# A fixed TensorE order for the attention of a two-block network: fillers, turns, values, next scores

## The chip, the cores and the metric

The kernel runs on one core of a Trainium2 chip. Its time is device microseconds for one execution, and the median over a few runs is what counts. Before the change the median was 1479.84 us (three runs, 1479.53 to 1481.19). The engines are named as the profile names them: PE is TensorE (matrix multiplies), DVE is VectorE, ACT is ScalarE, POOL is GpSimd, and SP is the engine that issues the loads.

## The reference

The network is two blocks of two layers each, on one sequence of 256 tokens with 1024 channels. The change touches the first block, whose two layers each compute this, cut to what matters:

```
mod = silu(c) @ ada_w + ada_b
sh_m, sc_m, gt_m, sh_f, sc_f, gt_f = split(mod, 6)
h = rms_norm(x) * (1 + sc_m) + sh_m
aq, ak, av, bq, ..., cqkv, cz, ca, cb = split(h @ w_in)
o_a = banded_attention(rope(aq), rope(ak), av, window 128, sinks)
o_b = nsa_mixer(...)        # compressed + selected + window branches, gated
o_c = gated_delta_net(conv(cqkv), ca, cb, cz)   # per chunk a solve, then a scan over chunks
x = x + gt_m * (concat(o_a, o_b, o_c) @ w_out)
h = rms_norm(x) * (1 + sc_f) + sh_f
x = x + gt_f * ((silu(h @ w_gate) * (h @ w_up)) @ w_down)
```

Every tensor is fp32. `ada_w` is 1024 x 6144 for each layer, so modulation is a product of one vector with a large matrix. Inputs pass through unchanged by the change described here; only the order of the work, its buffers and the engine of a few operations differ.

## The kernel before

**Splitting.** Every large fp32 product is computed as three multiplies of split parts (high by high, high by low, low by high). `cut` (L188) makes the two parts of a weight tile of 128x1024: `wh` by a copy on ACT (L193), and `wl` by a subtraction on DVE or POOL (L194). One projection block, `pf` (`proj_fm`, L209 to L211), is then 24 matmuls of 128x256 into PSUM.

**Loads.** `load` (L183) issues on SP. Nearly all weights go through one ring of three staging buffers named `ws`, 1 MB each. SP issues its loads in a fixed order, and a load whose staging buffer is still in use holds back all loads behind it.

**Modulation.** `mod_unit` (L342) loads 1 MB of `ada_w` into that same ring and reduces it on DVE with two operations of 128x1024 (L350). The units for layer 0 and 1 are done piece by piece by calls of `pump` among other work.

**The mixer of the first block** (`mixer1`) first makes the projections of seven heads while DVE, ACT, POOL and PE work on the triangular solve of the gated delta net. Then comes the attention. A pair of heads goes through: scores `sc` (L383, PE); maximum and exponentials `lg` (L394 on DVE, L399 on ACT) and the scaling by the reciprocal of the sum (L404 on DVE, L411 on ACT); three transposes for each head, `tp` (L419, PE), copied to SBUF as `pt` (L421, ACT); and the product with the values, `ot` (L429, L431, PE). There are six such pairs in a layer: two for banded attention (`aq0`, `aq1`), four for the window and selected branches (`bq0`, `bq1` against two key sets). Eight projection blocks (numbers 4 to 11 of `w_fm`) stand among them; each feeds a short convolution `gdn_conv` (copy `cu` L716, taps L725 to L730 on ACT and DVE, then transposes `vp` L736 or sums `ssp` L748 on PE). A projection `pz` (24 steps of 128x512, twice) ends the stage, and after it comes the scan over chunks (`gdn_scan`, first DVE instruction L879).

**What sets the order.** The framework's scheduler orders every engine's instructions by program position and readiness, so before the change the projection blocks are spread between the pieces of the attention wherever the scheduler found a place for them. Each engine executes its own list in order, and waits on semaphores of the others.

**Between the layers**, `begin1` normalizes the input of layer 1 with `norm`: for each of eight tiles `h = x * rb` (L303), scale and shift (L305 or L307), the high part `hh` (ACT, L308) and the low part `hl` (L309). POOL has seven of the multiplies and one `hl`.

Of the kernel before, what the change touches and what calls it, by code (L numbers as in the profile page):

```python
# [8 lines left out]
F32 = mybir.dt.float32  # L9
# [133 lines left out]
class Net:  # L143
# [44 lines left out]
    def cut(self, ws, pool=None, tag="w", bufs=6, eng=None):  # L188
# [34 lines left out]
    def proj_tm(self, outs, src, n, pre=None):  # L223

        mm = self.nc.tensor.matmul
        for k in range(0, KT, 2):
# [3 lines left out]
            for tb in range(2):  # L230
                t = slice(tb * P, tb * P + P)
                for i in range(2):
# [3 lines left out]
                    mm(outs[tb], lhsT=self.hh[k + i][:, t], rhs=wl[:, i, :], start=False, stop=last)  # L236

# [101 lines left out]
    def mod_load(self, l, u, sp=None):  # L339
        return self.load(self.io["ada_w"][l, u], (P, 2, 1024), sp, bufs=3 if sp is None else 4)  # L340

    def mod_unit(self, l, u, sp=None, aw=None):  # L342

        nc = self.nc
        if aw is None:
# [168 lines left out]
    def begin1(self, w_fm, pp):  # L514
# [3 lines left out]
        self.norm(range(KT), self.gmod[:, 1, 0, :], self.mod[:, 1, 0:8], range(1, 8), (5, 6, 7), (7,))  # L518
# [6 lines left out]
    def mixer1(self, l, begin, turn):  # L525
        nc, tc, io = self.nc, self.tc, self.io
        with ExitStack() as ctx:
# [11 lines left out]
            def conv(i0, blocks):  # L539
                for j, ps in enumerate(blocks):  # L540
                    if i0 > 2:
                        flush()
                    late.append(self.gdn_conv(l, sp, pp, g, i0 + j, ps))
                    if j % 2:
                        self.pump((3 if i0 == 4 and j == 1 else 1) if l == 0 and i0 > 2 else 0)
# [3 lines left out]
            conv(0, ahead)  # L549
# [62 lines left out]
            two = []  # L612

            def values():

                pts = [self.turned(sp, pp, u[1]) for u in two]
                self.pv([(out, pt, *rest) for (out, _, *rest), pt in zip(two, pts)])
                two.clear()


            bandq0, bandq1 = self.c(C_BAND, 128), self.c(C_BAND + 128, 256)
            for blk in range(2):
                ot = pp.tile([P, S], F32, tag="o", name="ot", bufs=1)
                sc = self.scores(pp, rot[f"aq{blk}"], self.kk[2])
                for half in range(2):
                    h = blk + 2 * half
# [953 lines left out]
```

## Time and profile before

| | |
|---|---|
| median of three runs | 1479.84 us |
| time of the profiled execution | 1485.39 us |
| its span | 1483.6 us |
| PE busy | 1416.1 us, 95% |
| DVE busy | 1137.7 us, 77% |
| ACT busy | 824.0 us, 56% |
| POOL busy | 122.5 us, 8% |
| mean granted TensorE clock | 0.98 |

The profiled execution has 1.8 us outside the span, and its time is 5.55 us above the median of the runs. The engines' busy time is an average over stages with different limits. The attention of layer 0 lies between about 105 and 198 us of the span, that of layer 1 between about 507 and 573 us, and the normalization at the start of layer 1 between about 424 and 446 us.

### The profile page before, as it was taken

The numbers are of one execution on the slowest core, as the hardware profiler recorded it, in microseconds if no ns is written. First come the engines' busy times: TensorE is split into PE (matmuls) and PEld (weight loads), VectorE is DVE, ScalarE is ACT, GpSimd is POOL, SyncE is SP. The second block draws the span as 40 slices with busy tenths as digits, with TensorE's granted clock in tenths as the row PEclk, the third lists the DMA queues.
The fourth block names the chain that finished last, engine by engine and source line by source line (L and its number), as shares of the span: only waits on it lengthen the run. The fifth ranks groups of instructions, "written<-read, shape, count | busy, mean of one in ns | idle before, by whom it ended". The sixth has DMA issues, their size and how long they took to land.

```text
span 1483.6 us, 29119 instructions
## 1 busy us (share of the span) xinstructions
PE 1416.1 (95%) x11742; PEld 1322.0 (89%) x11742; DVE 1137.7 (77%) x2352; ACT 824.0 (56%) x1585; POOL 122.5 (8%) x130
## 2 busy tenths in 40 slices
PE   5987999999999999999999999999999999899998
PEld 3865789999998778999999888899999888899997
DVE  7868789989868576975667886797888675887875
ACT  3634766445465586554446555665555654755554
POOL 0130101000042300100001001100000100100000
PEclk9997999999999999999999999999999999999999
DMA  9555457989732522779744443279664341655520
GB/s 374 200 199 212 168 192 296 359 312 346 287 105 93 200 86 103 271 264 160 285 163 146 142 143 142 99 277 228 249 230 139 116 144 56 252 214 201 187 86 29
DMA packets 52504, 287.77 MB, mean 194 GB/s; under 512 B 6061, under 2 KB 12081, under 8 KB 24466
## 3 DMA queue, kind: packets, MB, share of 16 engines
q1 hardware_dynamic: 50962, 279.62, 51.6%
q0 software_dynamic: 1408, 6.29, 3.5%
q8 instruction: 92, 1.51, 0.4%
q14 instruction: 42, 0.34, 0.1%
HBM read 277.97 MB, written 7.34 MB: 192 GB/s over the span
## 4 chain that ended last, share of the span: by engine, by line
PE 77%; DVE 12%; ACT 5%; issue 2%; POOL 2%; DMA 2%; POOLq 0%; SPq 0%; DVEq 0%; ACTq 0%
PE pf L209 15%; PE pf L210 14%; PE pf L211 14%; PE acc L209 5%; PE acc L211 5%; PE acc L210 5%; DVE ws L350 2%; DVE wl L194 2%; PE sc L383 2%; PE ot L429 2%; PE tp L419 1%; ACT wh L193 1%; DVE hl L205 1%; POOL sq L67 1%; PE zp L829 1%
## 5 line engine op out<-in xcount | busy, mean ns | idle before, releaser
L209 PE MATMUL pf<-hh,wh 128*128 128x256 f32 (+1 forms) x1976 | 566.8, 287 | 7.1 <-ACT wh L193 5.7
L210 PE MATMUL pf<-hl,wh 128*128 128x256 f32 (+1 forms) x1976 | 564.3, 286 | 6.3 <-DVE hl L205 6.3
L211 PE MATMUL pf<-hh,wl 128*128 128x256 f32 (+1 forms) x1976 | 562.6, 285 | 0.2 <-DVE wl L194 0.2
L194 DVE TENSOR_TENSOR wl<-ws,wh 128x1024 fp32r<-128x1024 f32 (+1 forms) x289 | 349.2, 1212 | 76.1 <-ACT wh L193 73.9
L193 ACT CAST wh<-ws 128x1024 fp32r<-128x1024 f32 (+1 forms) x299 | 306.8, 1036 | 180.6 <-PE pf L210 133.7
L209 PEld LDWEIGHTS pf<-hh,wh 128*128 128x128 f32 x1976 | 378.0, 192 | 15.2 <-ACT wh L193 6.5
L210 PEld LDWEIGHTS pf<-hl,wh 128*128 128x128 f32 x1976 | 378.6, 192 | 12.5 <-DVE hl L205 9.6
L211 PEld LDWEIGHTS pf<-hh,wl 128*128 128x128 f32 x1976 | 378.2, 192 | 2.4 <-issue 1.8
L211 PE MATMUL acc<-ah,dl 128*128 128x256 f32 x704 | 198.2, 282 | 0.0
L210 PE MATMUL acc<-al,dh 128*128 128x256 f32 x704 | 198.0, 282 | 0.0
L209 PE MATMUL acc<-ah,dh 128*128 128x256 f32 x704 | 197.7, 283 | 0.2
L194 DVE TENSOR_TENSOR dl<-wd,dh 128x1024 fp32r<-128x1024 f32 x88 | 107.6, 1223 | 50.6 <-ACT dh L193 50.3
L193 ACT CAST dh<-wd 128x1024 fp32r<-128x1024 f32 x88 | 91.9, 1049 | 94.4 <-PE acc L210 89.1
L210 PEld LDWEIGHTS acc<-al,dh 128*128 128x128 f32 x704 | 133.8, 190 | 0.2
L211 PEld LDWEIGHTS acc<-ah,dl 128*128 128x128 f32 x704 | 133.7, 190 | 0.0
L209 PEld LDWEIGHTS acc<-ah,dh 128*128 128x128 f32 x704 | 132.9, 190 | 0.7 <-ACT ah L201 0.6
L350 DVE SCALAR_TENSOR_TENSOR ws<-ws,sc 128x1024 f32<-128x1024 f32 x96 | 116.0, 1222 | 5.3 <-ACT sc L475 5.3
L67 POOL TENSOR_TENSOR sq<-sq 128x256 f32<-128x256 f32 x52 | 44.5, 855 | 774.0 <-ACT sq L65 768.3
L1119 DVE SCALAR_TENSOR_TENSOR fy<-fu,cw,fy 128x255 f32<-128x255 f32 (+1 forms) x176 | 84.1, 481 | 5.7 <-ACT fy L1117 3.0
L1100 DVE TENSOR_TENSOR a<-pf,rb 128x258 f32<-128x258 f32 x88 | 37.2, 424 | 32.2 <-PE pf L211 29.9
L399 ACT ACTIVATE lg<-lg,st 128x128 f32<-128x128 f32 x112 | 50.1, 449 | 21.2 <-DVE st L394 17.7
L1117 ACT ACTIVATE fy<-fu,cw 128x256 f32<-128x256 f32 x88 | 52.6, 599 | 12.1 <-DVE fu L1116 12.0
(370 smaller groups left out, 2143.3 us busy)
## 6 DMA issues: line engine op xcount, KB each, us to landing
ws<-in_ada_w SPq DMA_DIRECT2D x48, 1024.0 KB, 5.2
ws<-in_w_gu SPq DMA_DIRECT2D x44, 1024.0 KB, 5.2
wd<-in_w_dn SPq DMA_DIRECT2D x44, 1024.0 KB, 6.3
ws<-in_w_up SPq DMA_DIRECT2D x44, 1024.0 KB, 5.0
ws<-in_w_fm SPq DMA_DIRECT2D x16, 1024.0 KB, 5.1
ws<-in_w_even SPq DMA_DIRECT2D x12, 1024.0 KB, 4.9
w<-in_cmp_w SPq DMA_DIRECT2D x8, 1024.0 KB, 4.8
ws<-in_w_out SPq DMA_DIRECT2D x8, 1024.0 KB, 4.8
```

The source lines that it names most:

```text
L67: (nc.vector if i else nc.gpsimd).tensor_tensor(sq, sq, last, op=ALU.add)
L193: nc.scalar.copy(wh, ws)
L194: (eng or nc.vector).tensor_tensor(wl, ws, wh.bitcast(F32), op=ALU.subtract)
L209: mm(out, lhsT=lh, rhs=rh, start=start, stop=False, **kw)
L210: mm(out, lhsT=lh, rhs=rl, start=False, stop=False, **kw)
L211: mm(out, lhsT=ll, rhs=rh, start=False, stop=stop, **kw)
L350: nc.vector.scalar_tensor_tensor(a, a, 1.0, self.sc, op0=ALU.mult, op1=ALU.mult, accum_out=acc)
L383: self.nc.tensor.matmul(sc[half][:, out], lhsT=q[r, t], rhs=k[r, 0:n], start=True, stop=True)
L399: nc.scalar.activation(lg[:, rng[i]], lg[:, rng[i]], AF.Exp, bias=nm[:, i:i + 1], scale=-1.0, accum_out=den[:, i:i + 1])
L1100: nc.vector.tensor_tensor(t[j], ps[j], self.rb, op=ALU.mult)
L1117: nc.scalar.activation(y, u, AF.Identity, scale=w[:, 2:3], bias=w[:, 3:4])
L1119: nc.vector.scalar_tensor_tensor(y[:, d:S], u[:, 0:S - d], w[:, 2 - d:3 - d], y[:, d:S], op0=ALU.mult, op1=ALU.add)
```

## The change

The attention is written as six steps inside a region where the scheduler keeps PE's instructions in program order (`manual_schedule`). Each step is two fillers (a filler is a projection block of 24 matmuls, or a quarter of the two `pz` accumulations), then the turning of the pair's probabilities, the transposes of late convolutions, the values, and the next pair's scores. Modulation takes its 1 MB in two halves of 512 KB, through a ring `aw` of three buffers of its own; the ring of cut weights goes from six to five buffers, and the units are taken in another order. The compressed branch is split into its scores and its turning. In `begin1`, POOL multiplies three tiles and not seven, and no `hl`.

```
-    def cut(self, ws, pool=None, tag="w", bufs=6, eng=None):
+    def cut(self, ws, pool=None, tag="w", bufs=5, eng=None):
...
         for i in range(2):
             m = 2 * u + i
-            a, acc = aw[:, i, :], self.mod[:, l, m:m + 1]
+            a = self.load(self.io["ada_w"][l, u, :, i], (P, 1024), tag="aw") if aw is None else aw[:, i, :]
+            acc = self.mod[:, l, m:m + 1]
...
-        self.norm(range(KT), self.gmod[:, 1, 0, :], self.mod[:, 1, 0:8], range(1, 8), (5, 6, 7), (7,))
+        self.norm(range(KT), self.gmod[:, 1, 0, :], self.mod[:, 1, 0:8], (1, 3, 5), (5, 6, 7), ())
...
             self.cmp_mlp(l, sp, pp, g)
+            ws[4] = self.load_blocks(w_fm, 4)
             self.pump(2 if l == 0 else 0)
-            ws[4] = self.load_blocks(w_fm, 4)
...
+            def fills():
+                for i in range(4, 12, 2):
+                    for j, ps in enumerate(self.blocks(w_fm, i, pool=(1,), ws=ws.get(i))):
+                        late.append(self.gdn_conv(l, sp, pp, g, i + j, ps))
+                        yield
+                pz.extend(self.pj.tile([P, 512], F32, tag="pj", name="pz") for _ in range(2))
+                yield from self.proj_tm_steps(pz, io["w_z"][l], 512)
+
+            fill, pc = fills(), None
+            with tc.manual_schedule(engines={nc.tensor.engine}):
+                lgs = attend(0)
+                for i in range(6):
+                    for _ in range(2):
+                        next(fill)
+                    if i == 0:
+                        cmp = self.cmp_probs(sp, pp, g, raw)
+                    pts = [self.turned(sp, pp, lg) for lg in lgs]
+                    if i == 1:
+                        pc = cmp()
+                    for one in late[0:2 * min(i, 1)]:
+                        late.pop(0)()
+                    if i in (0, 1, 2, 4):
+                        ot = pp.tile([P, S], F32, tag="o", name="ot", bufs=1)
+                    value(i, pts, ot, pc)
+                    if i < 5:
+                        lgs = attend(i + 1)
+                        self.pump(2 if l == 0 else 0)
...
-        self.pump_list = [lambda l=l, u=u: self.mod_unit(l, u) for l in range(2) for u in range(8 * (1 - l), 24)]
+        units = [(0, u) for u in range(8, 20)] + [(1, u) for u in range(8)] + [(0, u) for u in range(20, 24)]
+        units += [(1, u) for u in range(8, 24)]
+        self.pump_list = [lambda l=l, u=u: self.mod_unit(l, u) for l, u in units]
```

Removed are the loops that computed the six pairs one after the other with their own `values()`, and `conv`, which took the projection blocks in two groups of four with one convolution behind each and pumped 2, 2, 3, 1, 1 and 1 units beside the 2 before them; `attend(i)` makes pair i's scores and probabilities, and `value(i, ...)` its products with the same calls as before.

Three places show what moved. The first is PE in layer 0, around the end of the first pair. Before, the pair's transposes (`tp`), the next scores (`sc`) and the values (`ot`) stand between single matmuls of a projection block (`pf`):

```order
L419 MATMUL tp<-ident,lg 128x128
L383 MATMUL sc<-kk_90,rotaq_802 128x128
L419 MATMUL tp<-ident,lg 128x128 x2
L383 MATMUL sc<-kk_90,rotaq_802 128x256
L211 MATMUL pf<-hh_72,wl 128x256
L209 MATMUL pf<-hh_73,wh 128x256
L429 MATMUL ot<-pt,vt_457 64x256
L431 MATMUL ot<-pt,vt_460 64x128 x2
```

On PE of the changed kernel, the same place and the end of the following step, the line numbers being those of the new source:

```order
L425 MATMUL tp<-ident,lg 128x128 x6
L435 MATMUL ot<-pt,vt_457 64x256 x2
L437 MATMUL ot<-pt,vt_460 64x128 x2
L389 MATMUL sc<-kk_90,rotaq_802 128x128 x2
L389 MATMUL sc<-kk_90,rotaq_802 128x256 x2
...
L425 MATMUL tp<-ident,lg 128x128 x6
L1055 MATMUL ctp<-ident,ce 64x128 x2
L751 MATMUL vp<-ident,cv 128x128 x4
L435 MATMUL ot<-pt,vt_457 64x256 x2
```

Between the two (at the line of dots) stand 48 `pf` matmuls without a break; all six transposes of a pair are together, and its four value products follow.

The second place is DVE in layer 0 after the first projection blocks. Before, the modulation operations (L350) of three units follow one another, with the compressed branch (`ce`) behind them:

```order
L350 SCALAR_TENSOR_TENSOR ws,mod<-ws,sc 128x1024
L730 SCALAR_TENSOR_TENSOR cv<-cu,cv 128x256
L202 TENSOR_TENSOR ol_123<-ot,oh_115 128x256
L730 SCALAR_TENSOR_TENSOR cv<-cu,cv 128x256
L350 SCALAR_TENSOR_TENSOR ws,mod<-ws,sc 128x1024 x2
L353 TENSOR_TENSOR mod<-mod,adab 128x2
L350 SCALAR_TENSOR_TENSOR ws,mod<-ws,sc 128x1024 x2
L353 TENSOR_TENSOR mod<-mod,adab 128x2
L350 SCALAR_TENSOR_TENSOR ws,mod<-ws,sc 128x1024
L1024 TENSOR_TENSOR ce<-cp,cs 128x64
```

On DVE of the changed kernel in the second step, L356 is the modulation, L409 and L410 are the sums and reciprocals of the probabilities, and L742 the taps of a convolution:

```order
L356 SCALAR_TENSOR_TENSOR aw,mod<-aw,sc 128x1024
L409 TENSOR_TENSOR st<-st 128x2
L403 TENSOR_SCALAR st<-st,nsink 128x2
L410 RECIPROCAL st<-st 128x2
L356 SCALAR_TENSOR_TENSOR aw,mod<-aw,sc 128x1024
L194 TENSOR_TENSOR wl<-ws,wh 128x1024
L359 TENSOR_TENSOR mod<-mod,adab 128x2
L356 SCALAR_TENSOR_TENSOR aw,mod<-aw,sc 128x1024
L409 TENSOR_TENSOR st<-st 128x2
L742 SCALAR_TENSOR_TENSOR cv<-cu,cw,cv 128x255
L410 RECIPROCAL st<-st 128x2
```

The modulation operations now stand singly between the pieces of the probabilities and the convolutions. From the first pair's probabilities to the scan's first instruction there are 20 of them before and 22 after; ahead of that stretch there are 20 before and 25 after.

The third place is SP's loads in the same stage. Before:

```order
L976 DMA w_1244<-in_cmp_w 128x2048
L185 DMA ws<-in_ada_w 128x2048 x2
L185 DMA ws<-in_w_fm 128x2x1024
L185 DMA ws<-in_ada_w 128x2048 x7
L185 DMA ws<-in_w_fm 128x2x1024
L185 DMA ws<-in_ada_w 128x2048
```

On SP of the changed kernel, where `aw` is the new ring and each of its loads is half as large:

```order
L185 DMA aw<-in_ada_w 128x1024 x6
L991 DMA w_1244<-in_cmp_w 128x2048
L185 DMA ws<-in_w_fm 128x2x1024
L185 DMA aw<-in_ada_w 128x1024
L185 DMA ws<-in_w_fm 128x2x1024
L185 DMA aw<-in_ada_w 128x1024 x3
L185 DMA ws<-in_w_fm 128x2x1024
```

The second load of projection weights stood behind seven loads of 1 MB in the same ring; it now stands behind one of 512 KB in another ring.

## Rows read from the trace of the kernel before

**Rows 1.** The page's first part: span, and busy time of each engine.

```profile
span 1483.6 us, 29119 instructions
PE 1416.1 (95%) x11742; PEld 1322.0 (89%) x11742; DVE 1137.7 (77%) x2352; ACT 824.0 (56%) x1585; POOL 122.5 (8%) x130
```

**Rows 2.** Busy time by stretches, layer 0's attention; columns in the first row.

```profile
core 0: us, PE busy (x) PEld busy (x) DVE busy (x) ACT busy (x) POOL busy (x), PEclk, DMA share, GB/s
120.00:130.00 10.00, 7.60 (x48) 5.42 (x47) 7.64 (x28) 6.76 (x25) 0.00 (x0) 1.00 0.60 205
130.00:140.00 10.00, 6.30 (x23) 3.64 (x22) 7.05 (x18) 4.05 (x12) 0.00 (x0) 0.52 0.36 125
140.00:150.00 10.00, 6.16 (x36) 5.87 (x37) 9.97 (x31) 3.36 (x7) 2.46 (x1) 0.62 0.88 337
150.00:160.00 10.00, 7.49 (x49) 6.51 (x49) 9.86 (x27) 6.73 (x19) 2.37 (x1) 0.89 0.75 265
160.00:170.00 10.00, 10.00 (x73) 8.52 (x71) 7.75 (x26) 7.36 (x23) 2.39 (x1) 0.94 0.69 220
```

**Rows 3.** PE's instructions in time: start, duration, engine, line; idle before, releaser.

```profile
128.43 0.84 PE L419 MATMUL tp<-ident,lg 128*128 128x128 f32 x3 [1.73 <-ACT lg L411]
143.69 0.58 PE L209 MATMUL pf<-hh,wh 128*128 128x256 f32 x1 [5.75 <-ACT wh L193]
...
145.44 0.41 PE L209 MATMUL pf<-hh,wh 128*128 128x256 f32 x1
145.66 0.41 PE L210 MATMUL pf<-hl,wh 128*128 128x256 f32 x1
...
150.78 0.28 PE L209 MATMUL pf<-hh,wh 128*128 128x256 f32 x1
150.90 0.28 PE L210 MATMUL pf<-hl,wh 128*128 128x256 f32 x1
...
156.55 0.33 PE L736 MATMUL vp<-ident,cv 128*128 128x128 f32 x1 [2.51 <-DVE cv L730]
```

**Rows 4.** ACT's instructions in time, at the weight cut that PE awaits.

```profile
142.59 1.99 ACT L193 CAST wh<-ws 128x1024 fp32r<-128x1024 f32 x2 [1.07 <-DMA ws<-in_w_fm]
```

**Rows 5.** SP's loads in time.

```profile
98.90 29.63 SPq L185 DMA_DIRECT2D ws<-in_ada_w  x7
137.65 0.38 SPq L185 DMA_DIRECT2D ws<-in_w_fm  x1
```

**Rows 6.** DVE's instructions in time: first probabilities, modulation, first of the scan.

```profile
106.80 0.27 DVE L394 CUSTOM_DVE_ANT_0 lg<-sc,cs 128x128 f32<-128x128 f32 x1
...
136.39 1.22 DVE L350 SCALAR_TENSOR_TENSOR ws<-ws,sc 128x1024 f32<-128x1024 f32 x1
...
141.12 1.22 DVE L350 SCALAR_TENSOR_TENSOR ws<-ws,sc 128x1024 f32<-128x1024 f32 x1
...
197.96 1.39 DVE L879 SCALAR_TENSOR_TENSOR dec<-qp,gcols,dec 128x128 f32<-128x128 f32 x5
```

**Rows 7.** Busy time by stretches: the whole attention of layer 0, then of layer 1.

```profile
106.80:197.96 91.16, 78.28 (x606) 61.66 (x601) 72.97 (x212) 58.39 (x164) 11.04 (x6) 0.89 0.56 194
507.15:573.00 65.85, 64.94 (x429) 50.70 (x428) 44.14 (x142) 53.24 (x149) 7.20 (x3) 1.00 0.34 121
```

**Rows 8.** DMA issues from 78 to 200 us: count, size, median us to landing.

```profile
ws<-in_ada_w SPq DMA_DIRECT2D x12, 1024.0 KB, 5.0
```

**Rows 9.** POOL's instructions in time, at the start of layer 1.

```profile
439.70 2.63 POOL L303 TENSOR_TENSOR h<-x,rb 128x256 f32<-128x256 f32 x2 [1.70 <-DVE hl L309]
```

**Rows 10.** PE's instructions in time, start of layer 1.

```profile
443.30 0.39 PE L234 MATMUL pm<-wh,hh 128*128 128x276 f32 x1 [1.82 <-ACT hh L308]
```

**Rows 11.** Busy time by stretches, elsewhere; columns as in rows 2.

```profile
440.00:450.00 10.00, 8.09 (x49) 7.44 (x48) 7.67 (x17) 8.73 (x18) 3.06 (x3) 0.83 0.18 54
470.00:480.00 10.00, 7.99 (x62) 7.38 (x61) 6.83 (x17) 2.36 (x6) 1.82 (x2) 0.83 0.03 6
```

**Rows 12.** PE's instructions in time, attention of layer 1.

```profile
516.29 0.33 PE L419 MATMUL tp<-ident,lg 128*128 128x128 f32 x1 [0.91 <-ACT lg L411]
```

More of the change, by code (lines that the diff above doesn't have):

```diff
@@ L336, in two_norms, with mod_load @@
         return gg, g1, e2
-    def mod_load(self, l, u, sp=None):
-        return self.load(self.io["ada_w"][l, u], (P, 2, 1024), sp, bufs=3 if sp is None else 4)
+    def mod_load(self, l, u, sp):
+        return self.load(self.io["ada_w"][l, u], (P, 2, 1024), sp, bufs=4)
     def mod_unit(self, l, u, sp=None, aw=None):
         nc = self.nc
-        if aw is None:
+        if aw is None and sp is not None:
             aw = self.mod_load(l, u, sp)
@@ L537, in flush @@
                     late.pop(0)()
[L539 to L545, printed above, removed]
             g = {"kT": [], "qT": []}
             g["ssq"], g["ssk"] = sp.tile([P, 8], F32, name="gssq"), sp.tile([P, 8], F32, name="gssk")
-            conv(0, ahead)
+            for j, ps in enumerate(ahead):
+                late.append(self.gdn_conv(l, sp, pp, g, j, ps))
             pre, ws = None, {}
@@ L609, in mixer1 @@
             self.cmp_mlp(l, sp, pp, g)
+            ws[4] = self.load_blocks(w_fm, 4)
             self.pump(2 if l == 0 else 0)
-            ws[4] = self.load_blocks(w_fm, 4)
[L612 to L626, printed above, removed]
-                    lg = self.probs(sp, sc[half], bandq0, bandq1,
-                                    nsink=self.nsink[:, l, h:h + 1], sink=self.sink[:, l, h:h + 1])
-                    r = slice(64 * half, 64 * half + 64)
-                    two.append((ot[r, :], lg, vt[0][:, r], vt[1][:, r], True, True))
-                values()
-                self.pump(2 if l == 0 else 0)
-                self.split(ot, oh[blk], ol[blk])
@@ L634, in mixer1 @@
-            conv(4, (ps for i in (4, 6) for ps in self.blocks(w_fm, i, pool=(1,), ws=ws.get(i))))
-            pc = self.cmp_probs(sp, pp, g, raw)
-            c0, c1 = self.c(C_CAUS, 128), self.c(C_CAUS + 128, 256)
-            for blk in range(2):
-                ot = pp.tile([P, S], F32, tag="o", name="ot", bufs=1)
-                nc.tensor.matmul(ot, lhsT=g["v2"][:, 2 * blk:2 * blk + 2, :].rearrange("p h d -> p (h d)"), rhs=pc,
-                                 start=True, stop=False, skip_group_check=True)
-                for br in range(2):
-                    sc = self.scores(pp, rot[f"bq{blk}"], self.kk[br])
-                    for half in range(2):
-                        h = 2 * blk + half
-                        r = slice(64 * half, 64 * half + 64)
-                        lg = self.probs(sp, sc[half], c0, c1, gate=g["gates"][:, :, 4 * (br + 1) + h])
-                        vs = slice(128 + 64 * br, 192 + 64 * br)
-                        two.append((ot[r, :], lg, vt[0][:, vs], vt[1][:, vs], False, br == 1))
-                    values()
-                self.split(ot, oh[2 + blk], ol[2 + blk])
@@ new lines, in value @@
+            def value(i, pts, ot, pc):
+                blk, br = divmod(i - 2, 2)
+                if i >= 2 and br == 0:
+                    nc.tensor.matmul(ot, lhsT=v2[:, 2 * blk:2 * blk + 2, :].rearrange("p h d -> p (h d)"), rhs=pc,
+                                     start=True, stop=False, skip_group_check=True)
+                two = []
+                for n, pt in enumerate(pts):
+                    r = slice(64 * n, 64 * n + 64)
+                    vs = r if i < 2 else slice(128 + 64 * br, 192 + 64 * br)
+                    two.append((ot[r, :], pt, vt[0][:, vs], vt[1][:, vs], i < 2, i < 2 or br == 1))
+                self.pv(two)
+                if i < 2 or br == 1:
+                    n = i if i < 2 else 2 + blk
+                    self.split(ot, oh[n], ol[n])
```

35 lines of the change are left out of this document (26 added, 9 removed).

## The prediction

> **What bounds the kernel now.** I read the page first: PE is busy 1416.1 of 1483.6 us [rows 1], so it idles 67 us in all, and a change in the order of its work can give back only part of that. Which part, the table of 10 us stretches tells. In layer 0's attention PE is busy 7.60, 6.30, 6.16 and 7.49 us of four stretches in a row [rows 2], 27.55 of 40, so 12.45 us of idle time lie there, the largest hole that the change touches. The reader should look at DVE in the same rows: it is at 7 to 7.6 us of ten while the hole opens and at 9.97 and 9.86 in its second half. It is late rather than free.
>
> PE's instructions in order of time say what ended the idle time [rows 3]: 1.73 us before a pair's transposes, until ACT had scaled the probabilities; 5.75 us before a projection block, until ACT had cut its weights; 2.51 us before the transposes of a convolution, until DVE had finished it. For the longest, one step back: ACT had waited for the load of those weights [rows 4]. SP's list shows why the load was late. Seven modulation loads were issued from 98.90 us on over 29.63 us, because each needs a staging buffer that DVE must first empty, and the projection weights went out only at 137.65 us [rows 5]. The operations that empty them are the five that start from 136.39 to 141.12 us, 1.22 us each [rows 6]. So PE waited for weights, and the weights for modulation.
>
> The hole has a second price. The granted clock is 0.52 and 0.62 in two of these stretches. The reader can see its price in the starts of matmuls of 128x256: 0.22 us apart after 145.44 us and 0.12 us after 150.78 us [rows 3]. Counting each stretch's busy time times what its clock lacks gives 6.30 x 0.48 + 6.16 x 0.38 + 7.49 x 0.11 + 10 x 0.06, about 6.8 us. A perfect order would thus save 12.45 + 6.8, some 19 us, if nothing else were late.
>
> **Part 1, layer 0's attention: -12 us (-15 to +3).** What is late next is DVE. From the first probabilities at 106.80 us to the scan's first DVE instruction at 197.96 us [rows 6] are 91.16 us, of which DVE is busy 72.97 and PE 78.28 [rows 7]. PE's work at full clock is 78.28 less 6.8, 71.5 us. DVE's grows: the order has 22 modulation operations where 20 stood, so 72.97 + 2 x 1.22 = 75.4 us. DVE has become the longer of the two, and how fully it can be used decides. Before, it was 72.97/91.16, 80% busy. Where it was the bound, from 140 to 160 us, it was 99% busy [rows 2]. The new order helps it: modulation has its own buffers, so an operation that finds its data ready fills DVE's gaps singly; the weights stand behind one half-load where they stood behind seven. But each pair is still a chain through PE, DVE, ACT and PE again, and DVE takes its list in order. I take 95%, nearer to the stretch where it was the bound: 75.4/0.95 = 79.4 us, so 11.8 us less. At 99% it is 76.2 (-15), at 80% 94.3 (+3). Both ends stay in the range.
>
> Three things in this part I cost at nothing beyond that. Five more modulation operations stand before the first probabilities (25 for 20), 6.1 us of DVE beside the solve; the trace has one such operation in a round of the solve without a longer round, and DVE's share above leaves room for the rest; if not, +2. The solve's last rounds lose the single projection matmuls that stood between them, which then follow in one piece. And 512 KB loads cost more issues on SP, which issues nothing else that is urgent there.
>
> **Part 2, layer 0's scan and output projection: +1 (-1 to +6).** About five modulation operations now stand among the scan's DVE instructions, which are themselves a chain with PE. At 1.22 us each [rows 6] that is 6.1 us if each delays the chain, nothing if each fits a wait. The scan has waits on PE in each round, so I take 1. Later modulation is the less by as many, for which I take -0.5 at the feed-forward part that follows, so +0.5 together.
>
> **Part 3, the start of layer 1: -2 (-3 to +1).** PE waits 1.82 us at 443.30 us for ACT's last high part [rows 10], which stands at the end of a chain through POOL: its two multiplies at 439.70 us take 2.63 us [rows 9]. The stretch is 1.91 us short of busy at a granted clock of 0.83 [rows 11], so wait and clock together are worth 1.91 + 8.09 x 0.17, 3.3 us. With three tiles on POOL the last tiles come from DVE. DVE gets four more multiplies and one more low part, at 7.67 us busy of ten [rows 11], which keeps a little of the wait. Were DVE the later of the two, it could cost 1.
>
> **Part 4, layer 1's attention: +3 (0 to +6).** There is nothing to win here: PE is busy 64.94 of 65.85 us at full clock, while DVE has 44.14 and ACT 53.24 [rows 7]. The single wait is 0.91 us at a pair's transposes [rows 12]. A fixed order can only add. In each step the six transposes wait for both heads' probabilities, and the whole queue of PE stands behind them (values, next scores, fillers); the scheduler had put a filler matmul there. The fillers of a step, 48 matmuls at 0.12 us, 5.8 us, cover a chain of DVE and ACT whose busy time is (44.14 + 53.24)/6 = 16 us a step, partly side by side; so the cover is not sure. A step that fails by the 0.91 seen costs 6 x 0.91 = 5.5 us. I take 0.5 a step, 3 us, as some steps will be covered.
>
> **Part 5, five buffers for cut weights and not six: 0 to +1**; elsewhere PE is at 95% and more, and a ring of five still holds two weight tiles beyond the one in use. I take +0.5.
>
> **Sum.** -11.8 + 0.5 - 2 + 3 + 0.5 = -9.8 us. The profiled execution took 1485.39 us, so the new one 1475.6; the median of the runs is 5.55 us under that, hence 1470.
>
> A rule of the skill speaks against part 1's small loads. The trace's 1 MB modulation loads landed after 5.0 us in the median [rows 8], and nothing here shows a load of half the size. The Trainium skill, "DMA: Bandwidth & Descriptors", section "Bandwidth", says to batch transfers to at least 1 MiB for three quarters of the peak; by its fit in the section "Anatomy of one DMA" (2.0 us and the bytes at 436 GB/s) two halves would take an estimated 6.4 us one after the other where one whole takes 4.4. By that rule the second rival below would be likelier; by the trace, in which the DMA engines are between 0.36 and 0.88 busy in these stretches, halves can overlap.
>
> **The rivals.**
>
> *DVE is not held by data but PE and ACT are held by each other (slower).* In layer 0's attention each engine waits for the next in a fixed circle, and DVE stays 80% busy: +3. Layer 1 loses its 0.91 at each step, +5.5; the other parts stay at -1. Together +7.5: 1487. For it speaks that PE's longest list now waits on one condition, and that a hole lowers the clock: a stretch with 7.99 us of PE's ten has a clock of 0.83 [rows 11]. Against it, that 120 to 130 us with 7.60 still has 1.00 [rows 2] and that fillers are now 48 in one piece. It decides, with layer 1 at +5.5, when DVE falls below 75.4/(91.16 - 4.5) = 87% of layer 0's stretch. The Trainium skill, "TensorE: Matmul & The Clock Gate", section "A second HAM failure mode: psum-queue depth-cycling", says that short idle times between groups of matmuls make the clock swing between its two levels; the two rows just named show it once and once not.
>
> *The ring of three halves paces modulation, or the weights stay late (no change).* A half is reduced in 1.22 us, but its buffer is full again only after a load, at most the 5.0 us of a whole one [rows 8]. Three in flight give one half per 1.67 us; a burst of four in a step would wait some 1.5 us, five steps 7.5 us of DVE. And the weights of blocks 4 and 5 do stand behind six half-loads. Layer 0 then gains 4.5 and the sum is -2.5: 1477.
>
> *Everything fits (larger gain).* DVE at 99%, -15; the scan 0; begin -3.3; layer 1 0: -18, 1462. For it speaks that ACT and PE have room in layer 0 (58.39 of 91.16 busy for ACT); against it, 99% over 90 us.
>
> **How the numbers follow.** The forecast has a chance of 0.50, the larger gain 0.18, the ring 0.20, the slower one 0.12. A measurement of this kernel cannot tell 0.2%, 3 us, from no change: faster is below 1476.9, slower above 1482.8. The forecast's own bounds (layer 0 -8 to -14, layer 1 0 to +5) are 1464 to 1476, faster in nearly all. The ring case is half on each side of 1476.9. So faster is 0.49 + 0.18 + 0.10 = 0.77, the same 0.01 + 0.10 + 0.01 = 0.12, slower 0.11. The range 1460 to 1480 holds the forecast, the ring and most of the larger gain, and leaves out the slower case and the gains beyond 20 us.
>
> **What would show it.** The first probabilities of layer 0 stay near 107 us and the scan's first DVE instruction comes at 186 us, with DVE 95% busy between and PE's clock near 1. No projection block waits 5 us for its cut weights, and SP issues the weights of the second pair of blocks well before they are cut. PE's waits move to `tp` and `ot`, up to 2 us each in layer 0. Layer 1's attention ends some 3 us later after its start, with short waits at `tp`. The wait of 1.82 us at `pm` is gone. The prediction is wrong if DVE shows holes of more than 1.5 us in front of modulation (then the ring paces it), if PE's clock stays below 0.9 in layer 0, or if layer 1 loses more than 6 us.

## The result: slower, and the profile after

The changed kernel takes 1490.88 us in the median (four runs, 1489.77 to 1496.11) against 1480.11 for the kernel before in the same comparison: a ratio of 1.007, 95% interval 1.0049 to 1.009. In a second comparison, beside other variants, it was 1.0062 (1.0045 to 1.0079). The forecast was 1470, faster; the time lies outside its range.

A second profile of each kernel was taken, since a single execution can mislead: the profile of before that stands ahead of the prediction is 5.5 us above the median of its runs, and a second one took 1476.23 us. The table gives both profiles of each kernel. The marks are the starts of DVE's first probabilities and of the scan's first DVE instruction, and the starts of PE's last matmuls of the output projections and feed-forward parts and of its first `pm` in layer 1.

| stretch | before, two profiles | after, two profiles | mean change | forecast |
|---|---|---|---|---|
| start to layer 0's first probabilities | 106.8, 106.5 | 113.9, 113.9 | +7.2 | 0 |
| from there to the scan | 91.2, 89.4 | 84.9, 83.5 | -6.1 | -11.8 |
| scan to the end of the output projection | 32.0, 32.0 | 36.0, 34.9 | +3.5 | +0.5, with what follows |
| layer 1: first `pm` to first probabilities | 73.1, 73.1 | 72.0, 71.7 | -1.3 | -2 |
| layer 1: probabilities to the scan | 65.3, 65.3 | 69.7, 69.7 | +4.4 | +3 |
| layer 1: end of output projection to end of feed-forward | 197.4, 193.4 | 200.6, 201.2 | +5.5 | +0.5 (five buffers) |
| second block, first probabilities to PE's end | 613.0, 609.8 | 606.4, 607.7 | -4.3 | 0 |

Two terms carry the miss: up to layer 0's scan the two first rows add to +1.1 where -11.8 was forecast, and the feed-forward row has +5.5 where +0.5 was. The -4.3 in the second block is in part that of one long execution of before (see e9).

The page's first part answers to [rows 1]; PE is still at 95%, so nothing of the loss is seen there.

```profile
span 1488.2 us, 29207 instructions
PE 1411.2 (95%) x11742; PEld 1320.1 (89%) x11742; DVE 1143.7 (77%) x2357; ACT 823.2 (55%) x1585; POOL 121.6 (8%) x125
```

The stretches show it. First layer 0's solve and attention by 10 us, then the whole attention of layer 0 and of layer 1 of the changed kernel; the columns are those of [rows 2].

```profile
100.00:110.00 10.00, 7.51 (x142) 6.19 (x138) 9.96 (x13) 5.64 (x14) 9.09 (x5) 0.91 0.95 346
110.00:120.00 10.00, 10.00 (x135) 8.24 (x133) 6.05 (x20) 2.08 (x5) 1.96 (x3) 0.50 0.49 156
140.00:150.00 10.00, 4.66 (x30) 3.66 (x29) 10.00 (x23) 7.31 (x24) 2.66 (x1) 0.79 0.60 199
150.00:160.00 10.00, 8.72 (x56) 6.42 (x55) 8.24 (x26) 6.55 (x21) 0.00 (x0) 0.70 0.45 171
160.00:170.00 10.00, 7.85 (x49) 5.39 (x48) 8.97 (x26) 7.46 (x21) 0.00 (x0) 0.83 0.90 325
113.90:198.85 84.95, 74.86 (x627) 60.84 (x628) 75.26 (x221) 56.87 (x168) 6.50 (x3) 0.87 0.66 232
512.71:582.41 69.70, 61.95 (x409) 50.59 (x409) 40.81 (x137) 51.65 (x147) 4.71 (x2) 0.90 0.27 93
```

The hole in layer 0 has moved, not closed: 4.66 us of PE from 140 to 150 us where [rows 2] had 6.16, and a new one in the solve from 100 to 110 us, with the clock at its lower level (0.50) for the 10 us behind it. Most of the new one is a single wait of PE for DVE:

```profile
106.42 0.37 PE L1012 MATMUL ckp<-hth,kw 128*128 128x16 f32 x2 [2.17 <-DVE hth L1007]
```

Layer 1, which had 0.91 us of idle PE at clock 1.00 [rows 7], now has 7.75 at 0.90. And DVE is as full as 9.96 and 10.00 where PE waits.

What DVE did in the new holes: its instructions in time, in the solve and in the attention's second step.

```profile
100.38 1.22 DVE L194 TENSOR_TENSOR wl<-ws,wh 128x1024 fp32r<-128x1024 f32 x1
101.51 3.38 DVE L356 SCALAR_TENSOR_TENSOR aw<-aw,sc 128x1024 f32<-128x1024 f32 x1
104.82 0.41 DVE L858 TENSOR_TENSOR xx<-xx,zp 128x256 f32<-128x256 f32 x1
106.55 3.38 DVE L194 TENSOR_TENSOR wl<-ws,wh 128x1024 fp32r<-128x1024 f32 x1
142.92 3.36 DVE L194 TENSOR_TENSOR wl<-ws,wh 128x1024 fp32r<-128x1024 f32 x1
146.27 1.21 DVE L356 SCALAR_TENSOR_TENSOR aw<-aw,sc 128x1024 f32<-128x1024 f32 x1
147.88 0.15 DVE L410 RECIPROCAL st<-st 128x2 f32<-128x2 f32 x1
```

Three operations took 3.36 to 3.38 us where operations of the same forms take 1.22: the cut at 100.38, and modulation in [rows 6]. POOL's instructions of the same times:

```profile
100.63 3.18 POOL L194 TENSOR_TENSOR wl<-ws,wh 128x1024 fp32r<-128x1024 f32 x1 [1.75 <-ACT wh L193]
103.76 2.40 POOL L849 TENSOR_TENSOR ms<-md,lv 128x256 f32<-128x256 f32 x2
106.45 2.40 POOL L194 TENSOR_TENSOR wl<-ws,wh 128x1024 fp32r<-128x1024 f32 x1 [0.29 <-ACT wh L193]
...
142.54 2.66 POOL L194 TENSOR_TENSOR wl<-ws,wh 128x1024 fp32r<-128x1024 f32 x1 [8.46 <-PE pf L211]
```

Each stretched operation starts while POOL cuts a weight and ends about one operation's own time (1.2 us) after POOL does: POOL ends at 103.81, 108.85 and 145.20, DVE at 104.89, 109.93 and 146.28. All three read both operands from SBUF. The operation at 104.82 reads one from PSUM (`zp`) and kept its 0.41 us beside POOL's next work. It goes the other way too: POOL's cut at 100.63 began while DVE made its own cut of 100.38, and took 3.18 us where the one at 106.45 took 2.40. The Trainium skill, "SBUF — State Buffer", section "Who interferes with whom", says that a DVE instruction with two SBUF inputs contends with a GpSimd instruction that reads SBUF, and that the second to come blocks until the first is done; these rows agree, with 2.2 us a time. It is a rule that the prediction should have weighed. The trace of before had it in small, an operation of 128x2 on DVE that took 2.33 us beside POOL's cut:

```profile
144.66 2.46 POOL L194 TENSOR_TENSOR wl<-ws,wh 128x1024 fp32r<-128x1024 f32 x1 [34.03 <-ACT wh L193]
...
144.81 2.33 DVE L113 TENSOR_TENSOR hl<-mod,hh 128x2 fp32r<-128x2 f32 x1
```

What stood behind: ACT's instruction that waits for the reciprocal, then PE's in layer 0 and layer 1.

```profile
148.13 0.80 ACT L417 ACTIVATE lg<-lg,st 128x128 f32<-128x128 f32 x2 [2.10 <-DVE st L410]
```

```profile
148.59 1.09 PE L425 MATMUL tp<-ident,lg 128*128 128x128 f32 x3 [4.93 <-ACT lg L417]
...
163.84 0.44 PE L751 MATMUL vp<-ident,cv 128*128 128x128 f32 x2 [1.12 <-ACT vs L752]
165.31 0.33 PE L751 MATMUL vp<-ident,cv 128*128 128x128 f32 x1 [1.02 <-ACT vs L752]
...
446.22 0.39 PE L238 MATMUL pm<-wh,hh 128*128 128x276 f32 x1 [0.51 <-ACT hh L313]
...
531.53 0.88 PE L425 MATMUL tp<-ident,lg 128*128 128x128 f32 x2 [2.01 <-ACT lg L417]
549.10 0.44 PE L751 MATMUL vp<-ident,cv 128*128 128x128 f32 x2 [2.00 <-ACT vs L752]
```

The chain in layer 0 reads: POOL's cut stretches DVE's cut by some 2.1 us, a modulation operation of 1.21 us and a convolution tap follow, the reciprocal of a head's sum comes at 147.88, ACT scales at 148.13, and PE, whose order has the transposes first, waited 4.93 us. Behind these transposes stood the pair's values, which need them, but also the next scores and 48 filler matmuls, which do not; the fillers' first weights were cut by 146.28, so they could have filled only the end of this wait. The wait of 5.75 us [rows 3] for cut weights is gone, as was forecast, and one of 4.93 stands in its place. In layer 1 the waits are the same without modulation, shorter and more of them. The wait at `pm` [rows 10] fell from 1.82 to 0.51.

### The profile page after: what moved, and what is told of

Same layout as the page of the kernel before. It is cut to its first block, busy times and chain, and to the rows that moved or that the text cites. A ratio compares the mean times of both kernels' runs of the same rounds, so it can differ in the third digit from the quotient of the medians.

```text
span 1488.2 us, 29207 instructions
## 1 busy us (share of the span) xinstructions
PE 1411.2 (95%) x11742; PEld 1320.1 (89%) x11742; DVE 1143.7 (77%) x2357; ACT 823.2 (55%) x1585; POOL 121.6 (8%) x125
## 4 chain that ended last, share of the span: by engine, by line
PE 73%; DVE 14%; ACT 6%; issue 3%; DMA 2%; POOL 1%; SPq 0%; POOLq 0%; DVEq 0%; ACTq 0%
PE pf L209 14%; PE pf L210 13%; PE pf L211 13%; PE acc L209 5%; PE acc L211 5%; PE acc L210 5%; DVE wl L194 3%; PE sc L389 2%; DMA ws<-in_w_gu 2%; PE zp L844 1%; ACT wh L193 1%; DVE hl L205 1%; PE ot L435 1%; DVE ws L356 1%; POOL sq L67 1%
## 5 line engine op out<-in xcount | busy, mean ns | idle before, releaser
L194 DVE TENSOR_TENSOR wl<-ws,wh 128x1024 fp32r<-128x1024 f32 (+1 forms) x289 | 355.9, 1233 | 93.2 <-ACT wh L193 91.3
L210 PE MATMUL acc<-al,dh 128*128 128x256 f32 x704 | 198.1, 282 | 0.9 <-DVE al L202 0.9
L193 ACT CAST dh<-wd 128x1024 fp32r<-128x1024 f32 x88 | 92.0, 1047 | 72.9 <-PE acc L210 71.1
L356 DVE SCALAR_TENSOR_TENSOR aw<-aw,sc 128x1024 f32<-128x1024 f32 x80 | 99.9, 1251 | 11.1 <-DMA aw<-in_ada_w 11.0
L1139 DVE SCALAR_TENSOR_TENSOR fy<-fu,cw,fy 128x254 f32<-128x254 f32 (+1 forms) x176 | 83.6, 480 | 5.4 <-ACT fy L1137 2.7
```

What stands on the lines that cost most here:

```text
L193: nc.scalar.copy(wh, ws)
L194: (eng or nc.vector).tensor_tensor(wl, ws, wh.bitcast(F32), op=ALU.subtract)
L210: mm(out, lhsT=lh, rhs=rl, start=False, stop=False, **kw)
L1139: nc.vector.scalar_tensor_tensor(y[:, d:S], u[:, 0:S - d], w[:, 2 - d:3 - d], y[:, d:S], op0=ALU.mult, op1=ALU.add)
```

## The experiments

Each is compared with runs of the kernel before on the same chip, and what is measured is given as the ratio to it with its interval. Three theories: A, modulation with buffers of its own runs too early and meets POOL's cuts; B, PE's fixed order; C, five buffers for cut weights.

**e1**, on the kernel after: whole units through the shared ring again.

```
-            a = self.load(self.io["ada_w"][l, u, :, i], (P, 1024), tag="aw") if aw is None else aw[:, i, :]
+            a = aw[:, i, :]     # aw = self.load(self.io["ada_w"][l, u], (P, 2, 1024)), ring ws
```

> The changed kernel with modulation loaded again as whole 1 MB units through the shared staging ring; the fixed order of TensorE stays. Theory A (early modulation): its own buffers let 25 modulation operations stand before layer 0's first probabilities and not 20, and two of DVE's 128x1024 operations there took 3.38 us and not 1.22, because POOL cut a weight at the same time. With 20 again, the first probabilities come at about 107 us and not 113.9, and the time falls from 1490.9 by some 6 us to about 1485. Theory B (fixed order): TensorE's waits behind transposes cost the time, in both layers; nothing of that changes here, and weights come late again, so the time stays at 1491 or rises.

Measured: 1.0007 (0.999 to 1.0024), some 9 us less than the changed kernel. The first probabilities came at 110.3 us, half of the way back. Layer 1 stayed at 69.2 us. A alone could have made this gain; B alone could not. Of A's two halves it is the earliness that this run speaks for: DVE operations beside POOL's cuts are still stretched (one modulation operation to 3.31 us at 135.67), but up to the last matmul of layer 0's output projection DVE makes 41 modulation operations, where the changed kernel makes 53 and the kernel before 42. That matmul starts at 222.9 us, in the changed kernel at 234.9 and 232.2; and the feed-forward part behind it, where the others are then made, takes 179.2 us, in the changed kernel 178.1 and 179.9.

**e2**, on after: PE's order left to the scheduler.

```
-            with tc.manual_schedule(engines={nc.tensor.engine}):
+            if True:
```

> The changed kernel with the same program order but with the scheduler free to order TensorE's instructions; modulation keeps its own buffers (25 operations before the first probabilities, 40 before the scan). Theory A: the solve of layer 0 stays as late as in the changed kernel (first probabilities at 113 us), and the time falls by no more than 3 us, to 1488 or above. Theory B: layer 1's attention is back at 65 us (first probabilities to scan) from 69.7, layer 0's gains as well, and the time falls by 6 to 10 us, to 1481 to 1485.

Measured: 0.999 (0.9966 to 1.0013), 12 us less. Layer 1's attention took 63.1 us. But the solve was as late as before (112.2 us, with the same two operations of 3.38 us). So B too takes back the whole loss; whether the two gains add, e7 asks.

**e3**, on after: no filler weight cut on POOL.

```
-                    for j, ps in enumerate(self.blocks(w_fm, i, pool=(1,), ws=ws.get(i))):
+                    for j, ps in enumerate(self.blocks(w_fm, i, ws=ws.get(i))):
```

> The changed kernel with every weight cut of the eight filler blocks made on DVE, none on POOL. Theory A: no DVE operation of 128x1024 is longer than 1.3 us any more; four more cuts of 1.22 us stand on DVE in each layer, but three stretched operations (2.2 us each beyond their own time, two in the solve and one in the attention) go, so the first probabilities come at about 110 us and the time falls by 3 to 6 us, to 1485 to 1488. Theory B: TensorE's order is the same and DVE has more to do, so 1491 to 1495.

Measured: 0.9996 (0.9983 to 1.001), 10 us less, more than A expected, and not where it expected it: the first probabilities came at 115.1 us, no earlier, and the attention behind them fell from 84.9 to 74.2 us. So the stretched operations are not shown to be what made the solve late. In the attention the gain is far more than the 2.2 us of one stretched operation, but it is not shown to be theirs alone: this order also has 19 modulation operations between the two marks where the changed kernel has 22, and fewer of PE's matmuls (569 for 627).

**e4**, on before: only modulation's own ring, and five buffers.

```
+            a = self.load(self.io["ada_w"][l, u, :, i], (P, 1024), tag="aw") if aw is None else aw[:, i, :]
...
-    def cut(self, ws, pool=None, tag="w", bufs=6, eng=None):
+    def cut(self, ws, pool=None, tag="w", bufs=5, eng=None):
```

> The kernel before, with only modulation's separate buffers added (halves of 512 KB in a ring of three, five buffers for cut weights and not six). It has 26 modulation operations before the first probabilities. Theory A: the solve is late by several us as in the changed kernel, and what the earlier weights give back in the attention is about as much, so 1480 to 1486, not faster than before. Theory B: separate buffers are the good half of the change: the wait of 5.75 us for the cut weights goes and the time falls below before, to 1470 to 1476.

Measured: 1.0049 (1.0027 to 1.0071), slower than before by 7 us, without any fixed order. The first probabilities came at 112.4 us, 5.7 later. The wait of 5.75 us for cut weights was gone, and from the first probabilities to the end of the output projection it took 117.1 us where before took 123.1 and 121.4; so layer 0 had won and lost about as much. The 7 us lie behind it: 71.3 us in layer 1's attention and 201.0 to the end of its feed-forward part, where e8, with five buffers alone, has 71.1 and 200.6. Against e8 the separate buffers made the kernel some 9 us faster; this run mixes the two edits and does not price them.

**e5**, the changed kernel again.

> The changed kernel unchanged, for a second profile and its time beside the variants. Both theories: 0.5 to 0.9% above the kernel before. If the stretched DVE operations in layer 0's solve (3.38 us beside POOL's weight cut, theory A) belong to the program and not to one execution, they stand there again, and the first probabilities come at 112 to 115 us.

Measured: 1.0062, first probabilities at 113.9 us. One operation in the solve took 3.38 us again (at 101.08); the second did not. In its place another was stretched beside POOL's cut, one that reads a single tensor, from SBUF; it took 0.23 us in the first profile:

```profile
105.97 2.14 DVE L1016 TENSOR_SCALAR hv<-hth 128x128 f32<-128x128 f32 x1
```

**e6**, on after: PE's order fixed in layer 0 only (`manual_schedule` where `l == 0`).

> The changed kernel with TensorE's order fixed in layer 0's attention and left to the scheduler in layer 1's. Theory A (early modulation, layer 0 alone): layer 1 costs nothing much, so at most 2 us less than the changed kernel, 0.5% or more above before. Theory B (fixed order, in both layers): layer 1's attention, first probabilities to scan, falls from 69.7 to 63 us as in the run with the scheduler's order in both, and the time by 5 to 7 us, to 0.1 to 0.3% above before; the rest of the loss stays in layer 0.

Measured: 1.0031 (1.0015 to 1.0048), 5 us less, layer 1's attention at 63.1 us as with the free order in both. B holds for layer 1.

**e7**, on after: e2 and e3 together.

> The changed kernel with TensorE's order left to the scheduler and all filler weights cut on DVE. Each edit alone took back the whole loss. If the two causes are apart (A in layer 0's solve and attention, B mostly in layer 1 and behind the transposes), the gains add in part: 5 us below each alone, 0.3 to 0.5% faster than before. If they are one (a stretched DVE operation hurts only because TensorE's fixed order lets it wait), the second edit adds nothing, 0 to 0.1% faster than before.

Measured: 0.9887 (0.9863 to 0.991), 1465.26 us in the median: faster than both kernels, and 16 us below the kernel before. The two gains add in full: 12 and 10 us alone, some 26 together. Layer 0's and layer 1's attention of this kernel:

```profile
110.50:173.20 62.70, 61.99 (x596) 52.52 (x595) 57.55 (x186) 50.26 (x152) 0.73 (x1) 1.00 0.61 212
494.60:556.80 62.20, 62.20 (x407) 49.28 (x408) 43.54 (x141) 51.16 (x148) 0.00 (x0) 1.00 0.33 115
```

PE is busy in all but 0.71 us, at full clock, with the program order of the change. (The scan's first instruction comes early here, among the last steps; up to the end of the output projection layer 0 takes 97.0 us from its first probabilities, 121.0 in the changed kernel. Part of that is paid back: the feed-forward part of layer 0 takes 185.2 us for 178.1.)

**e8**, on before: five buffers for cut weights, and nothing else (the second edit of e4).

> The kernel before with five buffers for cut weights instead of six and nothing else. Theory C (the smaller ring costs the feed-forward part of layer 1, which was 181 to 184 us in every variant with five and 179 before): 2 to 4 us slower than before, that stretch at 181 us or more. The others: no change within 0.1%, and the stretch stays at 179.

Measured: 1.0112 (1.0083 to 1.0141), 17 us slower, far more than C expected. The feed-forward part of layer 1 accounts for 2.5 (181.5 for 179.0); layer 1's attention for 5.8, with a PE clock of 0.88 that was 1.00 in [rows 7]:

```profile
517.50:588.60 71.10, 67.21 (x393) 52.75 (x394) 43.18 (x135) 50.06 (x142) 4.95 (x2) 0.88 0.26 91
```

The rest is spread over many places. With fewer buffers the scheduler writes another order on PE, DVE and ACT (the two profiles of before have one and the same). Whether that order costs the 17 us, or waits for a free buffer do, is not shown; but it is not a price of a buffer that could be carried elsewhere: with the free order of the change and five buffers, layer 1's attention takes 62 to 63 us.

**e9**, the kernel before again.

> The kernel before, for a second profile. Its first profile was 5.5 us above the median of its runs, and its second block (from the first probabilities of the block's first layer on) took 6 us more than the same instructions in all variants. If that was one execution, this profile's second block takes 607 us and not 613, and its span is 1475 to 1479; if it belongs to the program, both stay.

Measured: 1476.23 us, span 1474.5. The second block took 609.8 us, so about half of the difference belonged to that one execution. The other half stays open: kernels with five buffers took 606.4 to 609.3 us there, others with six 608.8 to 611.7.

**e11**, on e7: whole units through the shared ring, six buffers.

> The changed kernel with the scheduler's order, no cut on POOL, modulation in whole units through the shared ring, and six buffers for cut weights: what is left of the change is the program order of the attention (two fillers, turns, values, next scores) and the start of layer 1. If separate buffers are needed for the gain of e7, the weights come late again and the time is 0.3 to 0.8% below before, less than e7's 1.1%. If the program order makes the gain, 1.1 to 1.5% below before.

Measured: 0.9974 (0.9954 to 0.9995). Separate buffers (with five for cut weights in the bargain, e7) are worth some 13 us where the order is free and POOL does not cut: the same two edits cost 7 us in e4.

**e10**, on after, and **e12**, on e7: six buffers for cut weights and one for modulation's halves (`tag="aw", bufs=1`).

> The changed kernel with its fixed order and six buffers for cut weights, and one buffer for modulation's halves instead of three; this order has 20 modulation operations before the first probabilities as the kernel before has, and 33 before the scan. Theory B (fixed order): layer 1's attention, which has no modulation, stays at 69 to 70 us (first probabilities to scan), and the time at 0.1 to 0.4% above before, the gain being only layer 0's solve. Theory C (five buffers are the cost, in both layers): layer 1's attention falls to 65 us or less, and the time below before by 0.2% or more.

> As the last, but with modulation in halves through a ring of its own of one buffer. If separate buffers are what frees the weights, 1.1 to 1.5% below before, and faster than with the shared ring; if they only bring modulation forward, no better than the shared ring, 0.8 to 1.2%.

Measured: 1.0266 and 1.0187, slower by 40 and 28 us. Both expectations failed on a wait that neither named, which DVE had before 39 of the 80 halves. In e10:

```profile
DVE aw L356 <- DMA aw<-in_ada_w: 47.2, 39, 2.9
```

With one buffer, DVE stands at such a half until it has landed, and all its work behind. So the times say nothing on B or C. Layer 1's attention, which has no modulation, does: with six buffers it took 74.9 us in the fixed order and 67.0 in the free one (which also leaves POOL's cuts out), so there C, which expected 65 or less, fails, and the order costs with six buffers too. The times do show the rival of the pacing ring, at one buffer; in the changed kernel, with three, DVE waited so once from 60 to 200 us, for 1.7 us.

**e13**, on before, and **e14**, on e4: no filler weight cut on POOL.

> The kernel before with all filler weights cut on DVE, none on POOL. If POOL's cut beside DVE is a cost of its own, the two stretched stretches of DVE in layer 0's attention (at 144.8 and 151.9 us) go and pay for the four more cuts of 1.22 us: no change to 0.2% faster. If DVE's total is what counts, four cuts in layer 0 cost up to 4.9 us: 0.1 to 0.3% slower.

> The kernel before with modulation's separate buffers (five for cut weights) and all filler weights cut on DVE. With POOL's cut this was 0.5% above before. If the gain of the free order without POOL's cut (1.1% below before) comes from the program order of the attention, this stays above before or at it, 0 to 0.5% slower. If it comes from separate buffers together with no cut on POOL, 0.5 to 1.1% faster.

Measured: 0.9995 (0.9973 to 1.0017) and 1.0013 (0.9995 to 1.0032). POOL's cut costs the kernel before nothing, with separate buffers some 5 us, in the changed kernel 10, with the free order 15. And e14 has none of e7's gain. It differs from e15 below, which has 0.9933, by the program order of the attention and the order of the modulation units: the two together make 12 us, once PE is not held to the first.

**e15**, on e7: the start of layer 1 as before.

> The free order without POOL's cut, with the start of layer 1 as before (POOL multiplies seven tiles and has one low part). If that part of the change is worth 1 to 2 us, this is 1.0% below before where the other was 1.1%, and the wait of some 1.8 us at the last products of the start of layer 1 is back.

Measured: 0.9933 (0.991 to 0.9957) against 0.9887 for e7, so that part is worth some 7 us, but loosely known: the intervals just touch. The stretch from `pm` to the probabilities took 75.3 us and 72.4. The wait at `pm` itself stayed at 0.53 us with the old start: the gain comes later in that stretch, not at the wait that was forecast, and the fall of that wait in the changed kernel is not shown to be the work of POOL's three tiles.

**e16**, on e3: PE's order fixed in layer 0 only.

> The changed kernel without POOL's cut, TensorE's order fixed in layer 0 and free in layer 1. Fixed in both it was at the time of before; free in both, 1.1% below. If the fixed order costs each layer about as much, this lies half-way, 0.4 to 0.6% below before, with layer 1's attention at 62 to 63 us and layer 0's as with the fixed order in both.

Measured: 0.995 (0.993 to 0.997). With e3 and e7 at its sides, the fixed order costs 7 us in layer 1 and 9 in layer 0.

**e17**, on e3: the late convolutions' transposes behind the next pair's scores.

```
                     if i < 5:
                         lgs = attend(i + 1)
                         self.pump(2 if l == 0 else 0)
+                    for one in late[0:2 * min(i, 1)]:
+                        late.pop(0)()
```

> The fixed order in both layers without POOL's cut, with the late convolutions' transposes and sums moved behind the next pair's scores; before this move it was at the time of the kernel before (0.04% below). If TensorE's waits at those transposes (4.6 us in layer 1, 3.4 in layer 0, and the clock behind them) are the fixed order's price, values and next scores no longer stand behind them: layer 1's attention falls from 69 to 64 us and the time to 0.4 to 0.7% below before. If the price is the wait for the probabilities, no more than 0.2% below.

Measured: 1.0083 (1.0055 to 1.011), 13 us slower than e3. The waits went with the transposes (up to 3.12 us in layer 1), and new ones of 1.01 us in layer 0 and 1.32 in layer 1 came at the values, which now follow the turns at once and wait for their copy. So the first place of these transposes was not the price; it had covered that copy in part. Two places are tried and both leave waits; a third is not. These waits are not all of the 13 us: layer 0's output projection ends 10.4 us later than in e3, with 47 modulation operations before the scan for 44, and this is not divided further.

## Why the prediction was wrong

**What bounds the kernel: half right.** The hole in layer 0, its waits and the price of the clock were as read. But the step from the hole to its cause stopped too early: "PE waited for weights, and the weights for modulation" was true of one wait, and DVE, behind that modulation, had itself just waited for ACT, and so for the values that PE makes:

```profile
135.72 0.42 DVE L202 TENSOR_TENSOR ol<-ot,oh 128x256 fp32r<-128x256 f32 x1 [2.95 <-ACT oh L201]
```

Taking the load out of the circle (e4) gave some 5 us behind the first probabilities and cost 5.7 ahead of them.

**Part 1 failed twice.** The term of -11.8 measured -6.1: DVE was busy 75.26 of 84.95 us, 88.6% and not 95%. Its busy time was as counted (75.4), but some of it was blocking beside POOL. I had taken DVE's share to rise because work was always ready. What held it lower were its own waits, 7.2 us of them on PE, and some 3 on ACT:

```profile
DVE lg L400 <- PE sc L389: 4.3, 5, 1.2
DVE xx L858 <- PE zp L844: 2.9, 2, 1.8
```

With the order free and no cut on POOL (e7) DVE was busy 57.55 of 62.70 us, 92%, with fewer modulation operations there. The second failure is larger: "Three things in this part I cost at nothing", of which the first, five more modulation operations before the first probabilities, was bounded at +2. That stretch took 7.2 us more. e1, with 20 of them again, gets back 3.6, and the same step the other way, from e8 to e4, costs 3.5 (108.9 to 112.4 us). So half of the 7.2 is modulation's own ring, which was put at nothing. The two stretched operations there are 4.3 us of DVE time, but e3 removes them without a gain in this stretch (though it puts POOL's two cuts on DVE there). How the other half divides stays open; that PE's clock was 0.50 behind the first hole belongs to it.

One sum was missing behind both failures: the prediction counted the moved modulation by stretches (+2, then five at nothing, then about five at +1) and nowhere in all. It is 11 more operations up to the end of layer 0's output projection (53 for 42), at 1.22 us 13.4 us of DVE, in the part where it had just called DVE the bound.

**Part 2** was mis-sized: +3.5, within its bounds. There were six modulation operations in that stretch and not two; with one there (e1) it took 32.4 us, which fits the mechanism, modulation in the scan's chain, but was not tested apart.

**Part 3** may have come out by luck as far as the wait goes: it fell as forecast, but e15, with POOL's seven tiles, has 0.53 us there as well. The stretch fell by 1.3 us for 2 forecast.

**Part 4 was right in mechanism**, +4.4 for +3 and inside 0 to 6; e6, e16 and e2 show that it is the fixed order, 5 to 7 us against the free one. The cover I called "not sure" fails by up to 2.01 us at `tp`, and by 2.00 at `vp`, a wait that I had not listed; the clock of the stretch was 0.90. In layer 0 the cover failed by 4.93 us at `tp`, where up to 2 was the sign named.

**Part 5 failed**: "0 to +1". In the kernel before alone it is 17 us (e8). In the feed-forward part of layer 1, every kernel with five buffers has 181.3 to 183.5 us and every one with six 179.0; from the end of the output projection on it is 200.6 to 202.4 against 193.4 to 198.1. The argument was about how many tiles are in use; the number also changes the order that the scheduler writes, and which of the two costs is open.

**The rivals.** The slower one came at 0.12 with 1487. Its parts were there, PE and ACT held by each other and a lower clock, but its condition (DVE under 87%) was not met; the solve and the fewer buffers brought the rest. One of the prediction's signs of being wrong came true, a clock under 0.9 in layer 0 (0.87, in the second profile 0.90). The ring of three did not pace modulation: from 60 to 200 us DVE waited for a half once, for 1.7 us. The Trainium skill's rule on transfers under 1 MiB ("DMA: Bandwidth & Descriptors", "Bandwidth") did not decide either; the page gives it, and the fit that the prediction used, for transfers issued by GpSimd, and these are issued on SP. In the stretch of [rows 8] the halves landed after 5.2 us in the median, where the whole units had taken 5.0:

```profile
aw<-in_ada_w SPq DMA_DIRECT2D x30, 512.0 KB, 5.2
```

## What to carry to other kernels

A wait that ends last names the engine to look at, not the gain: before its whole length is counted, ask what that engine does next when the wait is gone, and with what it then collides. Work that is pulled forward is paid at the price of the stretch in which it lands, so count it there in all: the twelve operations that e1 moved back behind layer 0's output projection cost nothing measurable there. A fixed order on one engine holds only as well as the slowest step of the others; the same program order given as a priority to the scheduler was 16 us faster here (e3 against e7). And a buffer count is not a local edit where a scheduler reads it: measure it alone.

## What the runs showed of the hardware

In the rows shown here, a DVE operation with both operands in SBUF that began during a cut on POOL ended only about its own duration after POOL did: 3.38 us for 1.22, 2.33 for an operation of 128x2. So did one with a single operand in SBUF (2.14 us for 0.23, e5). With one operand in PSUM an operation kept its 0.41 us. A cut on POOL that began during DVE's took 3.18 us for 2.40. The profile counts the blocked time as busy. What such a collision costs depends on who waits for it: in the kernel before, taking POOL's cuts away changed nothing (e13).
